# Own places for each activation form, and the forms of a short-conv layer made in two parts

## The chip, the cores and the metric

The kernel runs on one core of one Trainium2 chip. The metric is the device time of one execution in microseconds (us); the lower the better. The core has five engines that this text names as the profile does: PE (matrix multiply; PEld is its weight load), DVE (vector), ACT (scalar and activation), POOL (GpSimd) and SP (which here only issues transfers). Each has its own queue of instructions and takes them strictly in order; an instruction that waits holds up all that stand behind it on the same engine. Transfers (DMA) are issued from SP's queue and, where a transfer adds to what is already in its target, from POOL's.

## The reference

A decoder trunk of two layers on 512 positions (T) of 2048 features, in float32, with a final RMS norm:

```python
for layer in range(DEPTH):                      # DEPTH = 2
    hn = rmsnorm(h, norm_w[layer])
    if layer % 2 == 0:
        h = h + hybrid_layer(hn, ...)           # DeltaNet heads and windowed attention
    else:
        h = h + shortconv_layer(hn, ...)
return rmsnorm(h, final_norm_w)

def shortconv_layer(h, w_in, conv_w, w_out):
    gate_b, gate_c, u, z = jnp.split(h @ w_in, 4, axis=-1)   # 4 x 3072 columns
    y = gate_b * causal_depthwise_conv(gate_c * u, conv_w)
    return (y * jax.nn.silu(z)) @ w_out
```

The change touches the seam between the two layers (the output projection of layer 1 and the input projection of layer 2) and the seam between layer 2's input and output projection.

## The kernel before

Features lie on the 128 partitions, so activations are 16 tiles of 128x512 (m or k = 0..15). A float32 product is made of three faster ones: an operand is split into a high part (`hi`, rounded, made by ACT) and the remainder (`lo`, made by DVE), and `mm3` issues hi·hi, hi·lo and lo·hi. Weights come in chunks of eight k tiles (128x1024, 512 KB): a load into `w_raw`, then `w_hi` on ACT and `w_lo` on DVE, three places each.

**Output projection of layer 1** (lines 787 to 837). For each of the 16 m tiles, PE accumulates 24 k tiles; `made` adds the residual tile `rx` (that gives h1), stores it to `H1d` in DRAM, squares it (`sq` on ACT) and adds the square to `ssq` on DVE, from which layer 2's norm factor comes. m = 14 and 15 run together as `last`, with k outside. Layer 2's own activation input is `hs`, h1 times the norm weight (`scaled`, ACT); the norm factor itself (`rbc`) is multiplied in later. For this factor PE makes two small products, `rs_ps` (from `ssq`) and, after a step on DVE and one on POOL (`rs_k`), `rs_pb`; a list of tasks with due times (`flow`) puts them between the products of the first pair.

**Input projection of layer 2** (lines 839 to 941). The 3072 channels are 24 tiles; for each tile two `pair`s make two of the four projections each. A pair splits positions and k tiles in two halves and makes its two outputs by seven products (0 to 6) instead of eight. A product is 24 matmuls of 128x256: for each of eight j one `fm` tile, that is a sum or difference of quarters of `hs[2j]` and `hs[2j+1]`, split into hi and lo. `forms` makes all seven `fm` tiles of a j (56 in all; each takes an ACT and a DVE step, and the sums `fa` to `fd` run on DVE). They stay in place for all 48 pairs. The order of products on PE is 0, 5, 6, 4, 1, 2, 3, into the banks acc, sb, sc, sb, acc, sb, sc. Their weights are five raw chunks q11, s1, s3, q12, q22, of which s1 and s3 each get a second load added to them by a transfer that POOL issues; product 0 uses q11, product 5 q11+s1, product 6 s3.

In `made`, the forms of j = 0, 1, 2 and 7 (m < 6 and m ≥ 14) come straight from h1. For j = 3 to 6 the kernel reads h1 back from `H1d` into `hr` (two places, shared with `sq`), while the last two m tiles are on PE: eight loads of 256 KB and eight `hs`.

**Places before.** Splits of layer 1's activations and half the forms share one set of 32 places ("x"), the rest of the forms 24 places ("x2"). The results of layer 2's mixer, `y`, go to `Y2d`; behind the last pair 23 of them are read back as `yl` (six places, shared with the channel tiles `ct`), split by `split_y` into places of "x" and "x2", and the final projection runs over them.

PE's order is the program's order. The order on the other engines is set by a scheduler at build time from the program's order and priorities (`high_priority` moves weight loads and splits ahead); on the chip it is fixed.

Of the kernel before, what the change touches and what calls it, by code (L numbers as in the profile page):

```python
# [7 lines left out]
F32 = mybir.dt.float32  # L8
# [23 lines left out]
NX2 = 24  # L32
NJ1 = 3
NRAW = 6
SPLIT_AHEAD = 600

# [38 lines left out]
def hybrid_trunk(ctx: ExitStack, tc: tile.TileContext, xT, w1, w1o, w2, w2o, nw, dcw, scw, hp, dnw, cst, msk, rope,  # L75
# [120 lines left out]
    def split_x(pool, tag, bufs, src, k, layer):  # L196
        hi = pool.tile([P, T], F32R, name="x_hi", tag=tag, bufs=bufs)
        lo = pool.tile([P, T], F32R, name="x_lo", tag=tag, bufs=bufs)
# [6 lines left out]
    with tc.tile_pool(name="ini", bufs=3) as ini:  # L205
# [11 lines left out]
        for k in range(KT):  # L217
# [5 lines left out]
            xs1.append(split_x(xp, "x", 32, xr, k, 0))  # L223
# [346 lines left out]
    with tc.tile_pool(name="dn", bufs=2, side="right") as dn:  # L570
# [166 lines left out]
        PX, PYD = (xp, "x", 32), (yd, "yd", 17)  # L737
        ys = [None] * KO

        def split_ready():  # L740
            for i, yt in enumerate(ytiles):
                if ys[i] is None and yt is not None:
                    ys[i] = split_y(PX if i < 16 else PYD, yt)
# [28 lines left out]
    def forms(pool, j, he, ho):  # L772
        e1, e2, o1, o2 = he[:, 0:H], he[:, H:T], ho[:, 0:H], ho[:, H:T]
        form(0, j, e1)
        fa, fb = (pool.tile([P, H], F32, name=n) for n in ("fa", "fb"))
        V.tensor_tensor(fa, e1, e2, op=ALU.subtract)
        V.scalar_tensor_tensor(fb, fa, -1.0, o2, op0=ALU.mult, op1=ALU.subtract)
        form(5, j, fb)
        form(4, j, fa)
        fc, fd = (pool.tile([P, H], F32, name=n) for n in ("fa", "fb"))  # L780
        V.tensor_tensor(fc, e2, o2, op=ALU.subtract)
        form(6, j, fc)
        form(1, j, o1)
        form(2, j, o2)
        V.tensor_tensor(fd, o1, fb, op=ALU.add)
        form(3, j, fd)

    with tc.tile_pool(name="op1", bufs=2, side="right") as op1:
# [50 lines left out]
    with tc.tile_pool(name="w4", bufs=1) as w4, tc.tile_pool(name="sc", bufs=1, side="right") as sc:  # L839
# [27 lines left out]
        def pair(wa, wb, c1, c2):  # L867
# [10 lines left out]
            with tc.high_priority(offset=SPLIT_AHEAD):  # L878
                w = split_w(q11)
            product(w, 0, a, True)  # L880
            a1 = sc.tile([P, H], F32, name="a1", bufs=2)
            A.activation(a1, a[:, 0:H], AF.Copy)
            with tc.high_priority(offset=SPLIT_AHEAD):
                V.tensor_tensor(q11, q11, s1, op=ALU.add)
                w = split_w(q11)
            product(w, 5, b, True)
            e = sc.tile([P, H], F32, name="e", bufs=2)
            V.tensor_tensor(e, b[:, 0:H], a1, op=ALU.add)
            with tc.high_priority(offset=SPLIT_AHEAD):
                w = split_w(s3)  # L890
            product(w, 6, c, True)
# [20 lines left out]
        def ctile(w=T):  # L912
            return sc.tile([P, w], F32, name="ct", tag="ct", bufs=6)

        rbc2 = sc.tile([P, T], F32, name="rbc2")
        for c in range(NCH):
# [3 lines left out]
            pair(w2[4 * c], w2[4 * c + 1], cc, u)  # L920
# [20 lines left out]
        ys = [None] * NCH  # L941
        for c in range(NCH):
            if c < NCH - 1:
                yl = sc.tile([P, T], F32, name="yl", tag="ct", bufs=6)
# [3 lines left out]
            ys[c] = split_y(PX if c < 16 else (x2p, "x2", NX2), yl)  # L948
# [129 lines left out]
```

## Time and profile before

| | us |
|---|---|
| median of 3 runs | 2817.7 |
| lowest and highest run | 2816.68 and 2822.33 |
| the profiled execution, its own time | 2821.6 |
| its span, first to last instruction | 2819.8 |
| PE busy | 2774.8 (98%) |
| DVE busy | 1798.9 (64%) |
| ACT busy | 1091.6 (39%) |
| POOL busy | 160.6 (6%) |

Times in the trace count from the start of the span. A matmul's start is firm; its end is modelled and overlaps the next one's start, so the distance between starts is what a matmul costs. An entry such as `[5.47 <-ACT w_hi L851]` says that the engine sat idle for 5.47 us before this instruction and that the instruction at line 851 of ACT released it. PEclk is the clock that PE was granted, as a share of 2.4 GHz.

### The profile page before, as it was taken

What the parts mean: (1) busy time and instruction counts of PE and PEld (TensorE: products, weight loads), DVE (VectorE), ACT (ScalarE), POOL (GpSimd) and SP (SyncE); (2) the same over time, 40 slices, a digit from 0 to 9 for tenths busy, and PEclk for the clock granted to TensorE, in tenths of its full rate; (3) what the DMA queues carried; (4) which work ended last, traced back from release to release, by engine and by line L of the source; (5) the groups of instructions that cost most, each with busy time, mean ns of one, the idle gap of its engine ahead of it and who ended that gap; (6) DMA issues with size and microseconds to landing.
All of it is one profiled execution on the core that took longest, in us unless ns stands there. A gap on an engine that the chain in (4) does not pass through costs nothing.

```text
span 2819.8 us, 41852 instructions
## 1 busy us (share of the span) xinstructions
PE 2774.8 (98%) x16648; PEld 2463.6 (87%) x16648; DVE 1798.9 (64%) x2707; ACT 1091.6 (39%) x1803; POOL 160.6 (6%) x226
## 2 busy tenths in 40 slices
PE   8999999999999999999999899999999999999998
PEld 6888888888887888888887899999999999997887
DVE  7766999555445655665334677777777777774223
ACT  5443444444432323234323444444444444443221
POOL 3110000000000000000000100000000000000000
PEclk9999999999999999999999999999999999999999
DMA  5655223322224333333444767776677676754333
GB/s 170 183 169 186 90 87 127 111 88 86 94 86 127 124 105 110 115 113 112 127 127 135 217 181 200 186 204 182 190 191 197 187 191 188 194 164 141 114 112 112
DMA packets 163059, 410.58 MB, mean 146 GB/s; under 512 B 41184, under 2 KB 55776, under 8 KB 162608
## 3 DMA queue, kind: packets, MB, share of 16 engines
q1 hardware_dynamic: 149040, 357.57, 39.4%
q0 software_dynamic: 13824, 50.34, 10.1%
q8 instruction: 131, 2.15, 0.3%
q14 instruction: 64, 0.52, 0.1%
HBM read 373.44 MB, written 34.41 MB: 145 GB/s over the span
## 4 chain that ended last, share of the span: by engine, by line
PE 93%; DVE 3%; DMA 2%; issue 1%; ACT 1%; SPq 0%; DVEq 0%; POOL 0%; ACTq 0%; POOLq 0%
PE acc L151 17%; PE acc L153 17%; PE acc L152 17%; PE sb L862 5%; PE sb L864 5%; PE sb L863 5%; PE sc L862 3%; PE sc L864 3%; PE acc L862 3%; PE acc L864 3%; PE sc L863 3%; PE acc L863 3%; PE p L96 2%; DMA w_raw<-in_w_dram 1%; DVE w_lo L146 1%
## 5 line engine op out<-in xcount | busy, mean ns | idle before, releaser
L151 PE MATMUL acc<-x_hi,w_hi 128*128 128x512 f32 x1536 | 622.5, 405 | 1.6 <-DVE cv_raw L319 1.6
L153 PE MATMUL acc<-x_hi,w_lo 128*128 128x512 f32 x1536 | 602.3, 392 | 5.1 <-DVE w_lo L146 5.1
L152 PE MATMUL acc<-x_lo,w_hi 128*128 128x512 f32 x1536 | 600.6, 391 | 0.5 <-DVE x_lo L200 0.3
L144 ACT ACTIVATE w_hi<-w_raw 128x1024 fp32r<-128x1024 f32 (+2 forms) x302 | 308.9, 1024 | 683.9 <-PE acc L152 513.9
L851 ACT ACTIVATE w_hi<-w_raw 128x1024 fp32r<-128x1024 f32 x336 | 356.3, 1061 | 559.2 <-PE acc L863 165.8
L146 DVE TENSOR_TENSOR w_lo<-w_raw,w_hi 128x1024 fp32r<-128x1024 f32 (+2 forms) x302 | 363.6, 1206 | 315.1 <-ACT w_hi L144 314.4
L853 DVE TENSOR_TENSOR w_lo<-w_raw,w_hi 128x1024 fp32r<-128x1024 f32 x336 | 411.0, 1224 | 160.9 <-ACT w_hi L851 159.0
L153 PEld LDWEIGHTS acc<-x_hi,w_lo 128*128 128x128 f32 x1536 | 289.2, 188 | 69.6 <-DVE w_lo L146 7.2
L151 PEld LDWEIGHTS acc<-x_hi,w_hi 128*128 128x128 f32 x1536 | 290.1, 189 | 57.4 <-DVE cv_raw L319 1.8
L152 PEld LDWEIGHTS acc<-x_lo,w_hi 128*128 128x128 f32 x1536 | 290.3, 189 | 55.8 <-DVE x_lo L200 1.8
L862 PE MATMUL sb<-fm,w_hi 128*128 128x256 f32 x1152 | 325.9, 283 | 0.0
L864 PE MATMUL sb<-fm,w_lo 128*128 128x256 f32 x1152 | 325.2, 282 | 0.0
L863 PE MATMUL sb<-fm,w_hi 128*128 128x256 f32 x1152 | 324.5, 282 | 0.0
L151 PE MATMUL acc<-y_hi,w_hi 128*128 128x512 f32 (+1 forms) x792 | 307.6, 388 | 4.8 <-ACT y_hi L732 3.2
L152 PE MATMUL acc<-y_lo,w_hi 128*128 128x512 f32 (+1 forms) x792 | 305.7, 386 | 3.5 <-DVE y_lo L734 3.5
L153 PE MATMUL acc<-y_hi,w_lo 128*128 128x512 f32 (+1 forms) x792 | 305.8, 386 | 1.2 <-DVE w_lo L146 1.2
L862 PE MATMUL sc<-fm,w_hi 128*128 128x256 f32 x768 | 218.0, 284 | 5.5 <-ACT w_hi L851 5.5
L862 PEld LDWEIGHTS sb<-fm,w_hi 128*128 128x128 f32 x1152 | 219.7, 191 | 0.0
L863 PEld LDWEIGHTS sb<-fm,w_hi 128*128 128x128 f32 x1152 | 218.9, 190 | 0.0
L864 PEld LDWEIGHTS sb<-fm,w_lo 128*128 128x128 f32 x1152 | 218.5, 190 | 0.0
L864 PE MATMUL sc<-fm,w_lo 128*128 128x256 f32 x768 | 217.5, 283 | 0.5 <-DVE w_lo L853 0.5
L863 PE MATMUL acc<-fm,w_hi 128*128 128x256 f32 x768 | 216.0, 281 | 1.3 <-DVE fm L769 1.3
(241 smaller groups left out, 4322.5 us busy)
## 6 DMA issues: line engine op xcount, KB each, us to landing
w_raw<-in_w_dram SPq DMA_DIRECT2D x428, 512.0 KB, 4.4
w_raw<-in_w_dram POOLq DMA_DIRECT2D x96, 512.0 KB, 7.1
w_raw<-in_w1o_dram SPq DMA_DIRECT2D x48, 512.0 KB, 3.6
w_raw<-in_w2o_dram SPq DMA_DIRECT2D x48, 512.0 KB, 3.6
Y2d<-y SPq DMA_DIRECT2D x23, 256.0 KB, 5.3
yl<-Y2d SPq DMA_DIRECT2D x23, 256.0 KB, 4.4
xr<-in_xT_dram SPq DMA_DIRECT2D x16, 256.0 KB, 4.3
KQd<-kq SPq DMA_DIRECT2D x8, 512.0 KB, 5.1
```

The source lines that it names most:

```text
L96: PE.matmul(o, lhsT, rhs, start=start, stop=stop)
L144: A.activation(hi, raw, AF.Copy)
L146: V.tensor_sub(lo, raw, hi.bitcast(F32))
L151: PE.matmul(acc, hi, xh, start=first, stop=False)
L152: PE.matmul(acc, hi, xl, start=False, stop=False)
L153: PE.matmul(acc, lo, xh, start=False, stop=last)
L851: A.activation(hi, src, AF.Copy)
L853: V.tensor_sub(lo, src, hi.bitcast(F32))
L862: PE.matmul(o, hi[:, j, :], xh, start=first and j == 0, stop=False, skip_group_check=not first)
L863: PE.matmul(o, hi[:, j, :], xl, start=False, stop=False, skip_group_check=not first)
L864: PE.matmul(o, lo[:, j, :], xh, start=False, stop=j == NJ - 1, skip_group_check=not first)
```

## The change

There are five edits. (1) Splits and forms get places of their own: for each of the seven forms eight places (`homes`), four sets in the pool that layer 1's splits use and three in the other. (2) `made` now makes forms 0, 5 and 6 (`EARLY`) for every pair of m tiles straight from h1, not only for four of them. Forms 4 and 1, and then 2 and 3 (`LATE`), are made in two passes over j = 0..6, both of which read h1 back: 28 `hr` loads and 28 `hs` in place of eight and eight. j = 7 has all seven forms made from h1 as before. (3) The first pair (`early`) runs products 0, 5 and 6 over j = 0..6 first and j = 7 of the three afterwards. (4) The store of h1 for m = 14 and 15 stands behind its square. (5) Channel tiles `ct` have four places instead of six, `yl` has three of its own, and the final splits take the places of forms 0, 5, 6, 4, 1, 2 in that order.

```diff
-NX2 = 24
-NJ1 = 3
+CT = 4
...
-    slots = iter([(x2p, "x2", NX2)] * NX2 + [(xp, "x", 32)] * 32)
+    EARLY, LATE = (0, 5, 6), (4, 1, 2, 3)
+    homes = [(x2p, "f0"), (xp, "x1"), (xp, "x2"), (xp, "x3"), (xp, "x0"), (x2p, "f1"), (x2p, "f2")]
...
-            if m < 2 * NJ1 or m >= KT - 2:
-                scaled(m, h1)
-                if m % 2:
-                    forms(op1, m // 2, hs[m - 1], hs[m])
-            SP.dma_start(H1d[m], h1)
+            scaled(m, h1)
+            if m % 2:
+                forms(op1, m // 2, hs[m - 1], hs[m], EARLY if m < KT - 1 else EARLY + LATE)
+            if m < KT - 2:
+                SP.dma_start(H1d[m], h1)
             sq = op1.tile([P, T], F32, name="sq1", tag="hr")
             A.activation(sq, h1, AF.Square)
             V.tensor_tensor(ssq, ssq, sq, op=ALU.add)
+            if m >= KT - 2:
+                SP.dma_start(H1d[m], h1)
...
-        for j in range(NJ1, NJ - 1):
-            for m in (2 * j, 2 * j + 1):
-                hr = op1.tile([P, T], F32, name="hr", tag="hr")
-                SP.dma_start(hr, H1d[m])
-                scaled(m, hr)
-            forms(op1, j, hs[2 * j], hs[2 * j + 1])
+        for which in (LATE[:2], LATE[2:]):
+            for j in range(NJ - 1):
+                for m in (2 * j, 2 * j + 1):
+                    hr = op1.tile([P, T], F32, name="hr", tag="hr")
+                    SP.dma_start(hr, H1d[m])
+                    scaled(m, hr)
+                forms(op1, j, hs[2 * j], hs[2 * j + 1], which)
...
+            else:
+                for js in (range(NJ - 1), range(NJ - 1, NJ)):
+                    for w, f, o in ((wa0, 0, a), (wb0, 5, b), (wc0, 6, c)):
+                        product(w, f, o, True, js)
...
-            return sc.tile([P, w], F32, name="ct", tag="ct", bufs=6)
+            return sc.tile([P, w], F32, name="ct", tag="ct", bufs=CT)
...
-                yl = sc.tile([P, T], F32, name="yl", tag="ct", bufs=6)
+                yl = sc.tile([P, T], F32, name="yl", bufs=3)
...
-            ys[c] = split_y(PX if c < 16 else (x2p, "x2", NX2), yl)
+            ys[c] = split_y(homes[FREED[c // 4]] + (NJ,), yl)
```

Line numbers move: what was line 831 (the `hr` load) is 842 in the changed kernel, 872 and 873 (the loads of q11 and s3) are 883 and 884, 870 (s1) is 881, 851 (`w_hi`) is 862, 795 (`hs`) is 803, 862 to 864 (the matmuls of a product) are 873 to 875.

The first place is SP's queue at the end of layer 1's output projection. Before, the last `hr` load stands ahead of q11 (line 872); s3 and seven more weight chunks come behind it, then the stores of h1:

```order
L831 DMA hr<-H1d 128x512
L872 DMA w_raw<-in_w_dram 128x1024
L873 DMA w_raw<-in_w_dram 128x1024
L875 DMA w_raw<-in_w_dram 128x1024
L876 DMA w_raw<-in_w_dram 128x1024
L870 DMA w_raw<-in_w_dram 128x1024
L872 DMA w_raw<-in_w_dram 128x1024
L873 DMA w_raw<-in_w_dram 128x1024
L804 DMA H1d<-rx 128x512 x2
```

In the changed kernel q11 (line 883) stands behind the 14th `hr` load and s3 (line 884) behind the 20th:

```order
L842 DMA hr<-H1d 128x512 x6
L883 DMA w_raw<-in_w_dram 128x1024
L842 DMA hr<-H1d 128x512 x6
L884 DMA w_raw<-in_w_dram 128x1024
L886 DMA w_raw<-in_w_dram 128x1024
L887 DMA w_raw<-in_w_dram 128x1024
L881 DMA w_raw<-in_w_dram 128x1024
L883 DMA w_raw<-in_w_dram 128x1024
L884 DMA w_raw<-in_w_dram 128x1024
L842 DMA hr<-H1d 128x512 x2
L817 DMA H1d<-rx 128x512 x2
L842 DMA hr<-H1d 128x512 x2
```

Two `hr` loads now stand behind s3 and five more chunks, and the last six (two of them shown) behind the stores; each `hr` load waits for the `hs` that read its place two loads earlier.

The second place is ACT's queue at the same point. Before, `w_hi` of q11 and of q11+s1 is followed at once by the scaling of m = 14 and 15 (`hs<-rx`) and their squares:

```order
L851 ACTIVATE w_hi<-w_raw 128x1024 x2
L795 ACTIVATE hs<-rx,nw_sb 128x512
L806 ACTIVATE sq_12784<-rx 128x512
L795 ACTIVATE hs<-rx,nw_sb 128x512
L806 ACTIVATE sq_12820<-rx 128x512
L768 ACTIVATE fm<-hs 128x256
L768 ACTIVATE fm<-fb 128x256
L768 ACTIVATE fm<-fa 128x256 x2
L768 ACTIVATE fm<-hs 128x256 x2
```

In the changed kernel the rows begin with the 21st `hs<-hr` and `w_hi` of s3; eight rows are left out, and then come the last `hs<-hr`:

```order
L803 ACTIVATE hs<-hr,nw_sb 128x512
L862 ACTIVATE w_hi<-w_raw 128x1024
...
L767 ACTIVATE fm<-fb 128x256
L803 ACTIVATE hs<-hr,nw_sb 128x512 x2
L803 ACTIVATE hs<-rx,nw_sb 128x512
L814 ACTIVATE sq_12928<-rx 128x512
L803 ACTIVATE hs<-rx,nw_sb 128x512
L767 ACTIVATE fm<-hs 128x256
L814 ACTIVATE sq_12964<-rx 128x512
```

The scaling of m = 14 and 15 and both squares now stand behind all 28 `hs<-hr`, and so behind all 28 loads; so do the forms of j = 7.

The third place is PE's order in the first pair. Before, `rs_ps` stands within product 5 (bank sb) and `rs_pb` within product 6 (bank sc):

```order
L863 MATMUL sb<-fm,w_hi 128x256
L864 MATMUL sb<-fm,w_lo 128x256
L96 MATMUL rs_ps<-cst_sb,ssq 128x128 x4
L862 MATMUL sb<-fm,w_hi 128x256
L863 MATMUL sb<-fm,w_hi 128x256
L864 MATMUL sb<-fm,w_lo 128x256
...
L864 MATMUL sc<-fm,w_lo 128x256
L96 MATMUL rs_pb<-cst_sb,rs_k 128x128 x4
L862 MATMUL sc<-fm,w_hi 128x256
```

In the changed kernel `rs_ps` stands between j = 0..6 of product 5 and j = 0..6 of product 6, and `rs_pb` ahead of the three j = 7:

```order
L874 MATMUL sb<-fm,w_hi 128x256
L875 MATMUL sb<-fm,w_lo 128x256
L95 MATMUL rs_ps<-cst_sb,ssq 128x128 x4
L873 MATMUL sc<-fm,w_hi 128x256
L874 MATMUL sc<-fm,w_hi 128x256
...
L875 MATMUL sc<-fm,w_lo 128x256
L95 MATMUL rs_pb<-cst_sb,rs_k 128x128 x4
L873 MATMUL acc<-fm,w_hi 128x256
L874 MATMUL acc<-fm,w_hi 128x256
L875 MATMUL acc<-fm,w_lo 128x256
L873 MATMUL sb<-fm,w_hi 128x256
```

The 21 matmuls of product 6 for j = 0..6 now all stand behind `rs_ps`, where only those of j = 6 and 7 of product 5 and the whole of product 6 did before.

## Rows read from the trace of the kernel before

**Rows 1.** The page: share of the chain that ended last, by engine.

```profile
PE 93%; DVE 3%; DMA 2%; issue 1%; ACT 1%; SPq 0%; DVEq 0%; POOL 0%; ACTq 0%; POOLq 0%
```

**Rows 2.** Window of the pairs: us; PE, PEld, DVE, ACT, POOL busy (x); PEclk, DMA, GB/s.

```profile
1600.00:2500.00 900.00, 900.00 (x7545) 900.00 (x7544) 696.50 (x831) 385.25 (x449) 80.07 (x112) 1.00 0.71 191
```

**Rows 3.** Waits of PE, 1545 to 1600.

```profile
PE sc L862 <- ACT w_hi L851: 5.5, 1, 5.5
PE acc L863 <- DVE fm L769: 1.3, 1, 1.3
```

**Rows 4.** Timeline of PE, 1549 to 1577: start, duration, line, tiles, idle before.

```profile
1549.73 0.39 PE L153 MATMUL acc<-y_hi,w_lo 128*128 128x512 f32 x1
1549.96 0.28 PE L862 MATMUL acc<-fm,w_hi 128*128 128x256 f32 x1
1550.07 0.28 PE L863 MATMUL acc<-fm,w_hi 128*128 128x256 f32 x1
...
1558.57 1.05 PE L96 MATMUL rs_ps<-cst_sb,ssq 128*128 128x128 f32 x8
```

**Rows 5.** Timeline of DVE, 1555 to 1576 (same columns).

```profile
1575.98 0.42 DVE L896 TENSOR_TENSOR b<-sb,a 128x256 f32<-128x256 f32 x1 [0.61 <-PE sb L864]
```

**Rows 6.** Windows of 1549.9 to 1600 (columns as rows 2).

```profile
1558.40:1565.20 6.80, 1.94 (x17) 1.73 (x16) 0.16 (x1) 0.50 (x1) 2.20 (x3) 1.00 1.05 311
1565.20:1572.00 6.80, 5.73 (x25) 5.43 (x26) 4.96 (x5) 2.88 (x5) 0.74 (x2) 0.50 1.02 255
```

**Rows 7.** Timeline of SP's queue, 1510 to 1575; one issue a row, or several (x).

```profile
1513.31 0.56 SPq L831 DMA_DIRECT2D hr<-H1d  x1
...
1529.30 0.33 SPq L831 DMA_DIRECT2D hr<-H1d  x1
...
1550.15 0.33 SPq L873 DMA_DIRECT2D w_raw<-in_w_dram  x1
...
1553.49 0.87 SPq L804 DMA_DIRECT2D H1d<-rx  x2
```

**Rows 8.** The tile hr, 1505 to 1560: its instructions and landings.

```profile
L795 ACT ACTIVATE hs<-hr,nw_sb x8: 705/717/725, 1516.4 to 1533.5; 128x512 f32<-128x512 f32 x8
...
DMA to landing us min/median/max: 2.5/3.0/4.7
```

**Rows 9.** The tile w_raw, 1539 to 1560: landings of its loads.

```profile
DMA to landing us min/median/max: 3.6/8.1/12.0
```

**Rows 10.** Timeline of ACT, 1548 to 1576.

```profile
1550.83 0.62 ACT L806 ACTIVATE sq<-rx 128x512 f32<-128x512 f32 x1
...
1564.70 2.95 ACT L851 ACTIVATE w_hi<-w_raw 128x1024 fp32r<-128x1024 f32 x3 [9.13 <-DMA w_raw<-in_w_dram]
```

**Rows 11.** Timeline of POOL, 1530 to 1580.

```profile
1560.39 1.35 POOL L188 TENSOR_TENSOR rs_k<-rs_t,mhalf 128x4 f32<-128x4 f32 x1
```

**Rows 12.** Waits of PE, 2500 to 2600.

```profile
PE acc L152 <- DVE y_lo L734: 3.5, 7, 0.9
PE acc L151 <- ACT y_hi L732: 3.2, 4, 1.3
```

**Rows 13.** Window of the final projection's first tile (columns as rows 2).

```profile
2526.57:2556.60 30.03, 23.26 (x75) 15.05 (x74) 20.56 (x31) 16.00 (x26) 0.00 (x0) 0.89 0.78 258
```

**Rows 14.** The tile yl, 2490 to 2560.

```profile
L732 ACT ACTIVATE y_hi<-yl x23: 612/630/634, 2522.2 to 2551.0; 128x512 fp32r<-128x512 f32 x23
L734 DVE TENSOR_TENSOR y_lo<-yl,y_hi x23: 684/689/695, 2523.2 to 2551.7; 128x512 fp32r<-128x512 f32 x23
...
DMA to landing us min/median/max: 2.7/4.4/6.7
```

**Rows 15.** Timeline of POOL, 1900 to 1950.

```profile
1905.59 0.44 POOL L918 MEMSET ct<- 128x2 f32 x1
1922.91 0.86 POOL L871 DMA_DIRECT2D w_raw<-in_w_dram  x1 [16.88 <-DMA w_raw<-in_w_dram]
```

**Rows 16.** Timeline of DVE, 1905 to 1924.

```profile
1911.39 0.74 DVE L928 SCALAR_TENSOR_TENSOR ct<-ct,scw_sb 128x512 f32<-128x512 f32 x1
```

More of the change, by code (lines that the diff above doesn't have):

```diff
@@ L194, in rstd_task, with split_x @@
         done.append(pb)
-    def split_x(pool, tag, bufs, src, k, layer):
-        hi = pool.tile([P, T], F32R, name="x_hi", tag=tag, bufs=bufs)
-        lo = pool.tile([P, T], F32R, name="x_lo", tag=tag, bufs=bufs)
+    def split_x(src, k, layer):
+        hi, lo = (xp.tile([P, T], F32R, name=n, tag=f"x{k // 4}", bufs=8) for n in ("x_hi", "x_lo"))
         A.activation(hi, src, AF.Copy, scale=nw_sb[:, layer, k:k + 1])
@@ L742, in split_ready @@
                 if ys[i] is None and yt is not None:
-                    ys[i] = split_y(PX if i < 16 else PYD, yt)
+                    ys[i] = split_y((xp, f"x{i // 4}", 8) if i < 16 else PYD, yt)
         flow.until(lambda: all(t is not None for t in ytiles[:KO - 2]))
@@ L761, in hybrid_trunk @@
     rd2 = []
-    slots = iter([(x2p, "x2", NX2)] * NX2 + [(xp, "x", 32)] * 32)
+    EARLY, LATE = (0, 5, 6), (4, 1, 2, 3)
+    homes = [(x2p, "f0"), (xp, "x1"), (xp, "x2"), (xp, "x3"), (xp, "x0"), (x2p, "f1"), (x2p, "f2")]
     fm = [[None] * NJ for _ in range(7)]
     def form(i, j, src):
-        pool, tag, bufs = next(slots)
-        t = pool.tile([P, 2, H], F32R, name="fm", tag=tag, bufs=bufs)
+        pool, tag = homes[i]
+        t = pool.tile([P, 2, H], F32R, name="fm", tag=tag, bufs=NJ)
         A.activation(t[:, 0, :], src, AF.Copy)
@@ L770, in form, with forms @@
         fm[i][j] = (t[:, 0, :], t[:, 1, :])
-    def forms(pool, j, he, ho):
+    def forms(pool, j, he, ho, which):
         e1, e2, o1, o2 = he[:, 0:H], he[:, H:T], ho[:, 0:H], ho[:, H:T]
-        form(0, j, e1)
+        if 0 in which:
+            form(0, j, e1)
         fa, fb = (pool.tile([P, H], F32, name=n) for n in ("fa", "fb"))
         V.tensor_tensor(fa, e1, e2, op=ALU.subtract)
[L777 to L786, printed above, removed]
+        if 5 in which or 3 in which:
+            V.scalar_tensor_tensor(fb, fa, -1.0, o2, op0=ALU.mult, op1=ALU.subtract)
+        if 5 in which:
+            form(5, j, fb)
+        if 6 in which:
+            fc = pool.tile([P, H], F32, name="fa")
+            V.tensor_tensor(fc, e2, o2, op=ALU.subtract)
+            form(6, j, fc)
+        if 4 in which:
+            form(4, j, fa)
+        if 1 in which:
+            form(1, j, o1)
+        if 2 in which:
+            form(2, j, o2)
+        if 3 in which:
+            fd = pool.tile([P, H], F32, name="fb")
+            V.tensor_tensor(fd, o1, fb, op=ALU.add)
+            form(3, j, fd)
     with tc.tile_pool(name="op1", bufs=2, side="right") as op1:
@@ L854, in split_w, with product @@
             return hi, lo
-        def product(w, f, o, first):
+        def product(w, f, o, first, js=range(NJ)):
             hi, lo = w
             o = o[:, 0:H]
-            for j in range(NJ):
+            for j in js:
                 flow.poll()
@@ L865, in product, with pair @@
                 flow.t += 0.36
-        def pair(wa, wb, c1, c2):
+        def pair(wa, wb, c1, c2, early=False):
             with tc.high_priority(offset=SPLIT_AHEAD):
@@ L919, in hybrid_trunk @@
             u = cu[:, 2:T + 2]
-            pair(w2[4 * c], w2[4 * c + 1], cc, u)
+            pair(w2[4 * c], w2[4 * c + 1], cc, u, c == 0)
             if c == 0:
```

32 lines of the change are left out of this document (20 added, 12 removed).

## The prediction

> **What bounds the kernel now.** I read the share of the chain first: PE holds 93% of it [rows 1]. Then PE's windows: over the 900 us of the pairs shown PE is busy for all 900, at full clock [rows 2]. So an edit can win or lose time only where PE waits, and I looked for these places in PE's waits. Two bear on the change.
>
> The first is the seam into layer 2. The first matmul of the first pair starts at 1549.96 [rows 4], and product 4, the fourth, has ended when DVE takes its bank at 1575.98 [rows 5]: 26.0 us. Matmuls of 128x256 start 0.11 to 0.12 us apart [rows 4]; four products of 24 at 0.12 us are 11.5 us, and the two small norm products take 1 us each (`rs_ps`, 1.05 [rows 4]). Some 12.5 us are lost here. In the waits, 5.5 of it is product 6 waiting for `w_hi` of s3, and 1.3 is a form of j = 7 [rows 3]; the rest is the clock, 0.50 from 1565.2 to 1572.0 behind the long wait, and before it [rows 6]. s3 is late because its load is issued only at 1550.15, when layer 1's last matmul gives its memory free [rows 7], and lands, with its second load added, for the `w_hi` at 1564.70 [rows 10].
>
> The second is the final projection's first tile. 75 matmuls of 128x512 take 30.03 us [rows 13]; such matmuls start 0.23 us apart [rows 4], so 17 us would do: 13 us are lost, in waits for `y_lo` and `y_hi` [rows 12] and in a mean clock of 0.89 [rows 13].
>
> **The change part by part.**
>
> *Fewer forms behind h1 of m = 15, and j = 7 put last.* It is meant for the 1.3 us wait, and removes it: j = 7 comes last. At most it gives 1.3 us [rows 3], if nothing else is late.
>
> *28 loads in place of eight.* This moves far more. Two places hold `hr`, and a load waits for the `hs` two before it, so the loads pace themselves. Before, eight were issued from 1513.31 to 1529.30 [rows 7], seven steps of 2.28 us. The floor is two in flight, landing in 2.5 us and read in 0.72 us [rows 8]: 1.6 us each; with the median landing of 3.0 us it is 1.9 us and some overhead. I take 2.1 us, since weight loads and a wait for the places of layer 1's splits fall into the first loads but not into those behind 1540; bounds 1.6 and 2.28.
>
> *s3 behind the 20th load.* The 20th is issued at 1513.3 + 19 x 2.1 = 1553.2, and s3 behind it, in SP's queue, 3 us later than before (0 at a rate of 1.6, 6.5 at 2.28).
>
> *The loads behind the weights.* The 21st and 22nd load stand behind s3 and five more chunks. Before, the issue of these six and what follows took from 1550.15 to 1553.49 [rows 7], 3.3 us, and a chunk took up to 12.0 us to land, where one alone took 3.6 us [rows 9]; the DMA engines were busy throughout (share 1.05 and 1.02) [rows 6]. Two more loads at the tail of six would be issued at about 1556.5 and land some 12 us later, at 1568.5, when s3 with its addition is there too. Bounds: 2.5 us, if they do not queue [rows 8], and 15 us.
>
> *The last six.* They go in three rounds of two, each round two times 2.1 us: 12.6 us. The 28th `hs` ends at about 1569.5 + 12.6 = 1582. Meanwhile PE has nothing: products 0 and 5 over j = 0..6 are 42 matmuls, 5 us, and their end at about 1557 to 1558 leaves PE at `rs_ps`, whose `ssq` needs the squares of m = 14 and 15; these stand on ACT behind the 28th `hs`. Product 6 stands behind `rs_ps` on PE, so it waits as well, although its weights and six forms are long there.
>
> *From the last `hs` to product 4's end.* Two `hs` and two squares on ACT (0.72 and 0.62 us each [rows 8, 10]) and the last addition to `ssq` on DVE: 3.5 us, 1585.5. `rs_ps`, 1 us. Then 21 matmuls of product 6: PE has stood still for some 28 us, and after 5.5 us it had 0.50 of its clock for 6.8 us [rows 3, 6], so at twice 0.12 us they take 5 us. `rs_k` on POOL (1.35 us [rows 11]) is hidden by them. `rs_pb` and nine matmuls of j = 7: 2 us. That makes 1593.5. The three places for split weights are held until j = 7 of the products, so product 4's `w_hi` (some 1 us: three in 2.95 [rows 10]) starts only as j = 7 of product 0 ends: 1 us more. 24 matmuls: 2.9 us. Product 4 ends at about 1597.5, against 1575.9 before: **+22 us**. With the low bounds throughout it is +8 (worked out under the rivals), with the high ones (s3 6.5 us late in place of 3, landings of 15 us, rounds of 4.6 us) some +30 to 33. Behind it nothing is late: the next pair's loads have 14 us of products 4, 1, 2 and 3 to arrive in.
>
> A page of the Trainium skill, "DMA: Bandwidth & Descriptors", section "Anatomy of one DMA — SWDGE (gpsimd) path", gives a transfer a fixed 2.0 us and its bytes at 436 GB/s. For 256 KB that is 2.6 us, and the lowest landing, 2.5 us [rows 8], agrees. By this rule alone all 28 loads would keep that pace and the sum would be the rival's +8. Its section "Queues, rings and completion order" says that an engine takes what a queue hands it in ring order, so that a load behind six chunks comes after their bytes; the landings of up to 12.0 us [rows 9] speak for the second rule here.
>
> *Own places for the final splits.* `split_y` starts when the first product of the last pair gives form 0 free, some 13 us before the first `y_hi` at 2522.2 [rows 14] (the last pair's six later products and a little more). But `yl` now has three places where it had six. A place is held for the landing (2.7 to 6.7, median 4.4), `y_hi` 0.63 and `y_lo` 0.69 [rows 14], with 0.3 us between: 6.0 us for three, 2.0 a tile. Three tiles are there early; the other 20 take 40 us from about 2509.5, to 2549.5, where the last `y_lo` ended at 2552.4 before. So **-3 us**. Bounds: 0, if loads of weights for the final projection and their splits on ACT stand in the way, and -13, the whole loss [rows 13], which needs landings near 2.7 us (1.45 us a tile, done at 2538).
>
> *ct with four places.* Four channel tiles a channel make each wait for its reader of the channel before. The nearest case is POOL's memset: at 1905.59 it ran a channel ahead, now it waits for line 928 on DVE, which ends at 1912.1 [rows 15, 16]. Queued behind it on POOL are the additions to weights; the next is issued at 1922.91 [rows 15]. 10 us of slack hide the wait: 0. Without it each of 23 channels could lose some us.
>
> *The rest* (more `hs` and forms inside the output projection, names of places for layer 1's splits): 0, with the 1.3 us of one late form [rows 3] either way.
>
> The sum on the profiled execution is 2821.6 + 22 - 3 = 2840.6. The runs' median lies 3.9 us below that execution's own time, so on the median it is 2817.7 + 19 = 2836.7. I predict 2837 us. A measurement of this kernel tells 0.2%, 5.6 us, from no change.
>
> **The rivals.**
> - *The forecast*: `hr` loads queue behind s3's group and the norm's squares behind all of them; 2829 to 2844.
> - *A slower chain*: the rate stays 2.28 us or worse, s3 goes out at 1557 or later, and each step behind it slips; middle +30, end 0 to -3: about 2847. For it speaks the rate before; against it, that DMA has little else to do from 1540 to 1550.
> - *Not slower*: behind s3 the loads land in 2.5 us. Issued at 1553.5, they give `hs` 21 and 22 at 1557.5, and three rounds of 2.5 + 1.4 us the 28th at 1569.2; `ssq` at 1572.7, product 6 at half clock to 1578.7, j = 7 to 1580.7, product 4 to 1584.5: +8. The same quick landings give `yl` its 1.45 us and the end its -11: 2815, no change that can be measured. It decides by the landing of the loads behind the six chunks; below 5 us it holds. Against it stand the 12.0 us [rows 9].
> - *Faster*: the early splits save all 13 us and the seam costs nothing: 2817.7 - 13 = 2805. That needs the squares of m = 14 and 15 by 1558, so 28 loads read by 1554.5, 1.5 us each without a stop; the lowest landings allow 1.6, and the queue behind s3 speaks against it.
>
> **How the numbers follow.** The forecast has 0.68, the slower chain 0.17, no change 0.09, faster 0.06. The two first are both slower: slower 0.85, same 0.09, faster 0.06. The likeliest one's own range is 2829 to 2844; for 8 in 10 I go from 2822 (the forecast with an end gain of 11 and 15 in the middle) to 2852 (the slower chain with no gain at the end).
>
> **What would show it.** In the profile of the changed kernel: PE idle for 20 us or more ahead of `rs_ps`, released by DVE's addition to `ssq`, in the waits near 1557 to 1586; `hr` landings of about 10 us for the 21st and 22nd load; a last `hs<-hr` near 1582; the clock at 0.50 behind it; the first `y_hi` near 2507 plus what the middle lost, and the last one only some us closer to the final projection's start than before. No PE wait between. I am wrong if PE's idle time ahead of `rs_ps` is below 10 us, if product 6 waits for forms, or if the channels show waits of their own.

## The result: 1.1% slower, and where the time went

The changed kernel takes 2850.4 us in the median (2848.74 to 2853.18) against 2817.6 for the kernel before: the ratio is 1.0114, with a 95% interval of 1.0097 to 1.0132. That lies at the upper edge of the predicted range of 2822 to 2852, on the side forecast, 13 us above the 2837 of the forecast, and above the 2829 to 2844 that the prediction gave its own theory. The changed kernel's profiled execution took 2848.74 us.

PE's waits of the changed kernel from 1500 to 1650 (engine, tile and line, what it waited for; total, times, longest) answer to [rows 3]:

```profile
PE rs_ps L95 <- DVE ssq L815: 30.6, 1, 30.6
PE sb L873 <- ACT w_hi L862: 3.4, 1, 3.4
PE sb L873 <- DVE e L913: 2.2, 1, 2.2
PE sb L875 <- DVE w_lo L864: 1.7, 1, 1.7
```

One wait of 30.6 us has come in: `rs_ps` for the squares of m = 14 and 15. The 5.5 us wait of product 6 for s3 is gone, since product 6 comes later than s3 now. The next three rows are small: product 5 waits 3.4 and 1.7 us, both ahead of the long wait, and product 4 2.2 us behind it.

Why the squares are late is in SP's queue (answering to [rows 7]) and ACT's (to [rows 8, 10]), here of the changed kernel:

```profile
1515.48 0.43 SPq L842 DMA_DIRECT2D hr<-H1d  x1
...
1545.79 10.25 SPq L842 DMA_DIRECT2D hr<-H1d  x6
1556.09 0.42 SPq L884 DMA_DIRECT2D w_raw<-in_w_dram  x1
...
1558.89 1.29 SPq L884 DMA_DIRECT2D w_raw<-in_w_dram  x1
1560.28 1.21 SPq L842 DMA_DIRECT2D hr<-H1d  x2
1562.42 1.63 SPq L817 DMA_DIRECT2D H1d<-rx  x2
1575.53 1.88 SPq L842 DMA_DIRECT2D hr<-H1d  x2
...
1580.94 4.51 SPq L842 DMA_DIRECT2D hr<-H1d  x4
```

```profile
1561.32 0.42 ACT L767 ACTIVATE fm<-fb 128x256 fp32r<-128x256 f32 x1 [1.49 <-DVE fb L793]
1574.78 0.72 ACT L803 ACTIVATE hs<-hr,nw_sb 128x512 f32<-128x512 f32 x1 [13.04 <-DMA hr<-H1d]
...
1580.19 1.35 ACT L803 ACTIVATE hs<-hr,nw_sb 128x512 f32<-128x512 f32 x2 [1.03 <-DMA hr<-H1d]
...
1583.71 1.39 ACT L803 ACTIVATE hs<-hr,nw_sb 128x512 f32<-128x512 f32 x2 [0.48 <-DMA hr<-H1d]
...
1588.89 0.72 ACT L803 ACTIVATE hs<-hr,nw_sb 128x512 f32<-128x512 f32 x1 [2.10 <-DMA hr<-H1d]
1590.27 0.72 ACT L803 ACTIVATE hs<-hr,nw_sb 128x512 f32<-128x512 f32 x1 [0.66 <-DMA hr<-H1d]
1590.90 0.71 ACT L803 ACTIVATE hs<-rx,nw_sb 128x512 f32<-128x512 f32 x1
...
1592.95 0.61 ACT L814 ACTIVATE sq<-rx 128x512 f32<-128x512 f32 x1
```

The reread loads go out from 1515.48, the 20th just ahead of s3 at 1556.09; the 21st and 22nd stand behind s3 and five chunks at 1560.28 and are read from 1574.78, after 13.04 us in which ACT did nothing; the other six take until 1590.27. Only then come the two `hs<-rx` and their squares. PE's `rs_ps` starts at 1594.52, 3.5 us after the last `hs<-hr` has ended; the clock granted from 1558.3 to 1599.2, a stretch in which PE is idle for most of the time, was 0.50 (columns as rows 2):

```profile
1558.30:1599.20 40.90, 9.10 (x41) 8.80 (x42) 17.46 (x43) 16.05 (x33) 4.67 (x6) 0.50 0.71 203
```

The wait shows in the chain of the whole execution too; on the page, `hr<-H1d` now holds 2% of it (a line of part 4):

```profile
PE acc L150 17%; PE acc L152 17%; PE acc L151 17%; PE sb L873 5%; PE sb L875 5%; PE sb L874 5%; PE sc L873 3%; PE acc L873 3%; PE sc L875 3%; PE acc L875 3%; PE sc L874 3%; PE acc L874 3%; PE p L95 2%; DMA hr<-H1d 2%; DMA w_raw<-in_w_dram 1%; PE o_ps L95 1%
```

The end, windows of the final projection's first tile in the changed kernel (columns as rows 2), and the tile `yl`, answering to [rows 13, 14]:

```profile
2556.36:2583.60 27.24, 21.67 (x75) 14.74 (x74) 16.25 (x24) 12.24 (x19) 0.00 (x0) 0.87 0.61 215
```

```profile
L730 ACT ACTIVATE y_hi<-yl x23: 613/629/634, 2537.4 to 2580.6; 128x512 fp32r<-128x512 f32 x23
L732 DVE TENSOR_TENSOR y_lo<-yl,y_hi x23: 683/686/694, 2539.3 to 2581.3; 128x512 fp32r<-128x512 f32 x23
...
DMA to landing us min/median/max: 2.6/3.5/5.2
```

The first tile's 75 matmuls take 27.24 us in place of 30.03; the first split starts 18.9 us ahead of the projection's first matmul (2537.4 against 2556.36), where it had started 4.4 us ahead. The last one is hardly earlier: 2580.6, 24.2 us behind that matmul, against 24.4 before.

Starts of PE's matmuls at a few marks split the profiled execution of each kernel into stretches; the medians are of all its runs. Matmul 200 is the start of PE's 200th matmul. Seam is from the first matmul of the first pair to the first of its fifth product; end is from the first matmul of the final projection's first tile to the first of its second.

| kernel | median, us | matmul 200 | start of the first pair | seam | end |
|---|---|---|---|---|---|
| before | 2817.6 | 57.8 | 1549.96 | 25.82 | 29.85 |
| changed | 2850.4 | 61.3 | 1550.59 | 56.81 | 27.06 |
| mid | 2853.0 | 64.4 | 1554.61 | 56.34 | 26.75 |
| one_pass | 2826.5 | 65.7 | 1559.62 | 28.93 | 27.72 |
| one_not_early | 2820.2 | 61.9 | 1552.18 | 25.22 | 27.14 |
| act_queue | 2856.2 | 63.3 | 1557.65 | 58.88 | 28.19 |
| reread_ahead | 2848.7 | 63.3 | 1554.09 | 55.83 | 27.81 |
| yl_shared | 2849.8 (one run) | 63.2 | 1553.32 | 56.16 | 25.75 |
| names_only | 2823.8 | 61.7 | 1554.84 | 25.69 | 28.17 |
| ct_yl_only | 2816.7 | 58.0 | 1549.39 | 25.85 | 25.63 |
| s3_later | 2820.4 | 58.4 | 1552.14 | 29.74 | 25.50 |
| stores_only | 2815.3 | 58.0 | 1547.24 | 25.31 | 25.28 |
| stores_first | 2809.2 | 58.0 | 1546.18 | 18.71 | 26.23 |

From before to changed the seam costs 31.0 us and the end gives back 2.8. The pairs in between give 1.8 us (922.02 us from the third pair's first matmul to the last pair's last, 920.19 in the changed kernel). The first pair starts 0.6 us later. These make 27.0 us, and the two profiled executions differ by 27.1 (2848.74 against 2821.6). The end is less certain than the seam, as it differs between traces of kernels with the same places there: 28.17 and 29.85 us with the places of before, 26.75 to 28.19 in the six with those of the changed kernel. The kernel before, run beside the others, had medians of 2817.6 to 2819.8.

### The profile page after: what moved, and what is told of

It reads as the page before. It is cut to its first block, busy times and chain, and to the rows that moved or that the text cites. A ratio compares the mean times of both kernels' runs of the same rounds, so it can differ in the third digit from the quotient of the medians.

```text
span 2846.9 us, 41954 instructions
## 1 busy us (share of the span) xinstructions
PE 2771.2 (97%) x16648; PEld 2459.8 (86%) x16648; DVE 1806.4 (63%) x2728; ACT 1111.4 (39%) x1831; POOL 161.2 (6%) x226
## 4 chain that ended last, share of the span: by engine, by line
PE 92%; DMA 4%; DVE 2%; ACT 1%; issue 0%; SPq 0%; DVEq 0%; POOL 0%; ACTq 0%
PE acc L150 17%; PE acc L152 17%; PE acc L151 17%; PE sb L873 5%; PE sb L875 5%; PE sb L874 5%; PE sc L873 3%; PE acc L873 3%; PE sc L875 3%; PE acc L875 3%; PE sc L874 3%; PE acc L874 3%; PE p L95 2%; DMA hr<-H1d 2%; DMA w_raw<-in_w_dram 1%; PE o_ps L95 1%
## 5 line engine op out<-in xcount | busy, mean ns | idle before, releaser
L873 PE MATMUL sc<-fm,w_hi 128*128 128x256 f32 x768 | 217.0, 283 | 0.0
L874 PE MATMUL sc<-fm,w_hi 128*128 128x256 f32 x768 | 216.4, 282 | 0.0
```

Of the source, the lines that this page charges most:

```text
L873: PE.matmul(o, hi[:, j, :], xh, start=first and j == 0, stop=False, skip_group_check=not first)
L874: PE.matmul(o, hi[:, j, :], xl, start=False, stop=False, skip_group_check=not first)
```

## The experiments

**mid**: all of `made` for m = 14 and 15 (scaling, forms of j = 7, squares, stores) moved between the two passes, so that the squares stand ahead of the second.

```diff
         for which in (LATE[:2], LATE[2:]):
             for j in range(NJ - 1):
...
+            if which == LATE[:2]:
+                for m, acc, rx in zip(last, accs, rxs):
+                    made(m, acc, rx)
-        for m, acc, rx in zip(last, accs, rxs):
-            made(m, acc, rx)
```

> The changed kernel with one move: m = 14 and 15 are scaled and squared between the two passes over the reread tiles, so their squares stand ahead of the second pass on ACT. Theory A (the second pass's 14 loads, put behind s3's group of weight chunks, are the cost, whoever waits for them): the 30.6 us wait of the norm product goes, but the second pass ends no earlier than 1590, and what needs it or stands behind it on ACT (the copy of product 0's bank, the forms of products 2 and 3) makes PE wait 20 us or more at product 4 or 2; 2840 to 2856. Rival B (only the place of the two squares on ACT is the cost): PE waits for s3 alone, as before the change; 2812 to 2822.

2853.0 us, ratio to before 1.0117 (1.0102 to 1.0132). PE's waits in mid, 1500 to 1650:

```profile
PE sb L874 <- DVE e L914: 28.2, 1, 28.2
PE sc L874 <- ACT w_hi L863: 9.2, 1, 9.2
```

`rs_ps` no longer waits. Product 4 waits 28.2 us instead, for `e`, which needs the copy of product 0's bank; that copy stands on ACT behind all 28 `hs<-hr`. The seam is as long as before the move (56.3 us). So the place of the squares is not the cost; the second pass is, and whatever stands behind it on ACT waits. Theory A holds, rival B falls.

**one_pass**: one pass that makes all four late forms, 14 loads.

```diff
-        for which in (LATE[:2], LATE[2:]):
+        for which in (LATE,):
```

> The changed kernel with one pass over the reread tiles that makes forms 4, 1, 2 and 3 together: 14 loads in place of 28, all of them ahead of s3 in SP's queue. Theory A (the number of loads and their place behind s3 are the cost): the last of them is read by about 1555, the norm product waits under 3 us, the seam loses about what it lost before the change, and the end keeps its 3 us; 2812 to 2822. Rival C (the order of the first pair with j = 7 last, and the split weights held for it, are the cost): still 2835 or more.

2826.5 us, ratio 1.0022 (1.0012 to 1.0033): 24 us below the changed kernel, and 4.5 above the upper end expected. PE's waits in one_pass, 1500 to 1650:

```profile
PE sc L873 <- ACT w_hi L862: 9.4, 1, 9.4
PE sb L873 <- DVE e L913: 2.2, 1, 2.2
...
PE rs_ps L95 <- DVE ssq L815: 0.3, 1, 0.3
```

`rs_ps` waits 0.3 us; the 30.6 us are gone with the second pass. The seam is bound by s3 again (9.4 us), and it still loses 3.1 us more than before, 2.2 of them at product 4, for `e`. The rest of the excess lies ahead of the first pair, which starts at 1559.6; but this profiled execution, of 2830.96 us, was the slowest of the eight.

**one_not_early**: one_pass, with products 0, 5 and 6 run whole in the first pair.

```diff
-            pair(w2[4 * c], w2[4 * c + 1], cc, u, c == 0)
+            pair(w2[4 * c], w2[4 * c + 1], cc, u)
```

> The changed kernel with one pass over the reread tiles and with products 0, 5, 6 in the first pair run whole again, j = 7 in its turn, not last. Theory H (with s3 as the bound of the seam, putting j = 7 last buys nothing): the seam from the first matmul of the pair to the end of the fourth product stays within 2 us of the 28.9 us of the one-pass kernel, or gets shorter by up to 3, since the places of split weights and the copy of bank acc come free before s3 arrives; 2821 to 2828. Rival I (j = 7 last is what keeps PE fed): 3 us or more longer; 2829 to 2834.

2820.2 us, ratio 1.0004 (0.9995 to 1.0013), below what was expected. The seam is 25.2 us, 3.7 shorter than in one_pass, where up to 3 was expected. PE's waits, 1545 to 1600:

```profile
PE sc L873 <- ACT w_hi L862: 6.9, 1, 6.9
PE acc L874 <- DVE fm L768: 0.9, 1, 0.9
PE acc L873 <- ACT fm L767: 0.8, 1, 0.8
```

The forms of j = 7 cost 1.7 us in all, as the 1.3 us of [rows 3] did, but they lie in time that is lost to s3 anyway (6.9 us). With j = 7 last, the split weights of three products are held and the copy of bank acc comes after the wait for s3. Theory H holds, rival I falls: beside one pass, edit 3 costs time.

**names_only**: the kernel before with other names for the same places.

```diff
-            xs1.append(split_x(xp, "x", 32, xr, k, 0))
+            xs1.append(split_x(xp, f"x{k // 4}", 8, xr, k, 0))
...
-                    ys[i] = split_y(PX if i < 16 else PYD, yt)
+                    ys[i] = split_y((xp, f"x{i // 4}", 8) if i < 16 else PYD, yt)
...
-    slots = iter([(x2p, "x2", NX2)] * NX2 + [(xp, "x", 32)] * 32)
+    slots = iter([(x2p, "x2", NX2)] * NX2 + [(xp, f"x{i // 8}", 8) for i in range(32)])
...
-            ys[c] = split_y(PX if c < 16 else (x2p, "x2", NX2), yl)
+            ys[c] = split_y((xp, f"x{c // 4}", 8) if c < 16 else (x2p, "x2", NX2), yl)
```

> The kernel before with nothing changed but the names of the 32 places that layer 1's splits and half the forms share: four sets of eight, in the same rotation, so that every tile keeps the place it had. At build time the scheduler orders the first 50 us otherwise with these names (as it does in the changed kernel). Theory F (this order costs the changed family its 3.4 to 7.8 us in the first 60 us): PE's 200th matmul starts at 61 to 66 us, in place of 58.1, and the whole is 2820 to 2826. Rival G (those us are differences between single executions): start near 58, 2817 to 2820, no change.

2823.8 us, ratio 1.0018 (1.0009 to 1.0027): 5.1 us slower, 2.5 to 7.6 by the interval. Windows of 20 to 60 us (columns as rows 2), first of the kernel before, then of names_only, then of the changed kernel:

```profile
20.00:60.00 40.00, 38.51 (x175) 30.88 (x176) 32.41 (x43) 21.27 (x36) 13.98 (x12) 1.00 0.49 168
```

```profile
20.00:60.00 40.00, 36.31 (x158) 28.74 (x159) 28.67 (x34) 19.51 (x34) 14.75 (x12) 0.96 0.48 165
```

```profile
20.00:60.00 40.00, 37.66 (x160) 30.01 (x161) 28.84 (x36) 20.02 (x34) 14.76 (x12) 0.93 0.50 170
```

In the same 40 us PE issues 175 matmuls in the kernel before, 158 with the new names, 160 in the changed kernel. By the rotation of the names no tile has another place or another reader. The order on PE is the same; the scheduler puts loads and splits of the first 50 us in another order on SP, ACT and DVE, and some later ones too, near 880, 1275 and 1530 us. Theory F's own mark is the 200th matmul: 61.7 us in place of 57.8, where 61 to 66 was expected. By that mark all traces fall into two groups: 57.8 to 58.4 us in the five kernels with the old names, 61.3 to 65.7 in the eight with the new ones. Theory F holds.

**ct_yl_only**: the kernel before with edit 5's places alone.

```diff
-            return sc.tile([P, w], F32, name="ct", tag="ct", bufs=6)
+            return sc.tile([P, w], F32, name="ct", tag="ct", bufs=4)
...
-                yl = sc.tile([P, T], F32, name="yl", tag="ct", bufs=6)
+                yl = sc.tile([P, T], F32, name="yl", bufs=3)
```

> The kernel before with one part of the change: four places for channel tiles and three of their own for the reread mixer tiles. Theory A: no channel waits (PE idle between 1600 and 2500 stays at 0); the splits start where they did, and three places instead of six make the final projection's first tile 0 to 4 us longer; 2817 to 2822. Rival D (the four places hold up weights on POOL or DVE in each channel): 2825 or more.

2816.7 us, ratio 0.9986 (0.9976 to 0.9996). PE does not wait between 1600 and 2500, so four channel places cost nothing. The end is shorter by 4.2 us in the traces, where 0 to 4 longer was expected, and by the interval the whole is 1.1 to 6.8 us faster than the kernel before. The tile `yl` in ct_yl_only:

```profile
L732 ACT ACTIVATE y_hi<-yl x23: 614/630/637, 2508.0 to 2549.0; 128x512 fp32r<-128x512 f32 x23
...
L945 SPq DMA_DIRECT2D yl<-Y2d x20: 319/320/565, 2509.7 to 2546.3; - x20
```

The first split starts at 2508.0, 14.2 us earlier than in [rows 14], with the forms in their old, shared places. So what held the splits back was `yl`'s wait for channel tiles; the forms' own places were not needed for it.

**yl_shared**: the changed kernel with seven places shared by channel tiles and `yl`.

```diff
-CT = 4
+CT = 7
...
-                yl = sc.tile([P, T], F32, name="yl", bufs=3)
+                yl = sc.tile([P, T], F32, name="yl", tag="ct", bufs=CT)
```

> The changed kernel with channel tiles and reread mixer tiles in one set of seven places, in place of four and three. Theory J (three places of its own set the pace of the reread): up to seven tiles are in flight once the last channel is done, and the first tile of the final projection takes 20 to 25 us in place of 27.1. Rival K (waiting for the channel tiles' places costs more than the depth gives, as in the kernel before): 28 to 31 us. The seam stays as in the changed kernel (56 to 57 us), the whole at 2842 to 2854.

The end takes 25.75 us, between what the theory and the rival expected, and 2849.8 us in one run. The splits start only at 2554.0 here (the row below), 4.4 us ahead of the projection, and the end is still 1.3 us shorter than in the changed kernel. That is one trace, and the end with three places of their own ranges over 1.4 us among the traces above, so the run doesn't settle how much depth buys beside an early start. It does show that sharing takes the early start away.

```profile
L730 ACT ACTIVATE y_hi<-yl x23: 612/617/636, 2554.0 to 2581.1; 128x512 fp32r<-128x512 f32 x23
```

**act_queue** and **reread_ahead** ask what makes the second pass slow. act_queue issues the reread loads from ACT:

```diff
-                    SP.dma_start(hr, H1d[m])
+                    A.dma_start(hr, H1d[m])
```

> The changed kernel with the 28 reread loads issued from ACT's queue instead of SP's; nothing else in the order of the squares changes. s3's load no longer stands behind the 20th reread load and goes out near 1550.5 instead of 1556.1. Theory A with the queue as cause of the long landings: loads 21 and 22 land in under 8 us instead of 14, the last is read near 1578 to 1583, PE's wait shrinks by 7 to 12 us; 2838 to 2844. Rival E (the DMA engines' bandwidth sets the landing, whichever queue): the landings stay at 12 us or more, and only the 5 us of the earlier start are won or nothing; 2845 to 2852.

2856.2 us, ratio 1.0131 (1.0116 to 1.0146): no faster than the changed kernel (1.0097 to 1.0132, so whether it is slower stays open), and above both expectations. The pair itself starts 7 us later than in the changed kernel; s3 went out at 1557.84, right behind its first matmul (1557.65). The wait of `rs_ps` is 27.8 us. The landings of the reread loads, of the changed kernel and of act_queue:

```profile
DMA to landing us min/median/max: 2.5/3.3/14.8
```

```profile
DMA to landing us min/median/max: 2.6/4.0/8.7
```

The longest landing is 8.7 us, where the changed kernel has 14.8. But each load now waits in ACT's queue for the work ahead of it, and the last `hs<-hr` starts at 1598.9, 41 us behind the pair's first matmul, against 40 in the changed kernel.

reread_ahead raises the loads over the weights:

```diff
-                    hr = op1.tile([P, T], F32, name="hr", tag="hr")
-                    SP.dma_start(hr, H1d[m])
-                    scaled(m, hr)
-                forms(op1, j, hs[2 * j], hs[2 * j + 1], which)
+                    with tc.high_priority(offset=2 * SPLIT_AHEAD):
+                        hr = op1.tile([P, T], F32, name="hr", tag="hr")
+                        SP.dma_start(hr, H1d[m])
+                        scaled(m, hr)
+                with tc.high_priority(offset=2 * SPLIT_AHEAD):
+                    forms(op1, j, hs[2 * j], hs[2 * j + 1], which)
```

> The changed kernel with the reread loads, their scaling and their forms at a higher priority than the weights: in SP's queue the 21st and 22nd load then stand behind s3 and two chunks, not five. Theory A with the queue (a load lands only behind the chunks that stand ahead of it): these two land after 7 to 11 us in place of 14, the norm product's wait shrinks from 30.6 to 23 to 28 us; 2841 to 2848. Rival P (the bytes in flight set the landing, in whatever order they were issued): 13 us or more, the wait within 2 us of 30.6; 2848 to 2854.

2848.7 us, ratio 1.0113 (1.0099 to 1.0127). SP and ACT in reread_ahead:

```profile
1559.36 0.42 SPq L886 DMA_DIRECT2D w_raw<-in_w_dram  x1
...
1561.19 2.31 SPq L843 DMA_DIRECT2D hr<-H1d  x2
1563.55 0.67 SPq L883 DMA_DIRECT2D w_raw<-in_w_dram  x1
...
1568.40 0.96 SPq L843 DMA_DIRECT2D hr<-H1d  x2
```

```profile
1567.65 1.36 ACT L803 ACTIVATE hs<-hr,nw_sb 128x512 f32<-128x512 f32 x2 [2.16 <-DMA hr<-H1d]
...
1579.68 0.72 ACT L803 ACTIVATE hs<-hr,nw_sb 128x512 f32<-128x512 f32 x1 [4.53 <-DMA hr<-H1d]
```

Loads 21 and 22 stand behind three chunks now and are both read by 1569.0, so the first lands within 6.5 us of its issue. But 23 and 24, issued at 1568.40 behind the other three chunks and the stores, are read only from 1579.68 on. The wait of `rs_ps` stays at 29.7 us. So the theory was right on the landing and wrong on the wait and the time, and rival P the other way round: what stands ahead in the queue sets which load is late, and moving it saves nothing that can be measured. My reading, which no run isolates, is that the eight loads behind s3 have to come through beside the same chunks in either order.

**s3_later**, **stores_only** and **stores_first** go on from ct_yl_only to the seam's own bound, s3. s3_later runs product 6 after 4 and 1 in the first pair:

```diff
-            with tc.high_priority(offset=SPLIT_AHEAD):
-                w = split_w(s3)
-            product(w, 6, c, True)
+            if not late6:
+                product6()
...
+            if late6:
+                product6()
+                V.tensor_tensor(c2[:, H:T], c[:, 0:H], b2, op=ALU.subtract)
...
-            pair(w2[4 * c], w2[4 * c + 1], cc, u)
+            pair(w2[4 * c], w2[4 * c + 1], cc, u, c == 0)
```

> The kernel before with four channel places and three of their own for the reread mixer tiles (as in ct_yl_only), and with product 6, the one that needs s3, run after products 4 and 1 in the first pair. Theory L (s3's late landing is the bound of the seam in the kernel before): product 6's wait of 5.5 us shrinks below 2 us, its half clock goes with it, and the first four products take 4 to 8 us less; 2807 to 2813. Rival M (weights of the other products arrive as late, all being loaded behind layer 1's last matmul): the wait moves to product 4 or 1; 2814 to 2818.

2820.4 us, ratio 1.0004 (0.9995 to 1.0013), above both expectations. Product 6 no longer waits, but product 4 waits 12.3 us for `e`:

```profile
PE sb L862 <- DVE e L888: 12.3, 1, 12.3
```

ACT in s3_later shows why:

```profile
1572.98 0.38 ACT L882 ACTIVATE a<-acc 128x256 f32<-128x256 f32 x1 [5.12 <-DMA H1d<-rx]
```

The copy `a` of product 0's bank waits for the stores of h1: its memory is that of the `rx` tiles, which the stores still read. Theory L is right that s3 held product 6, and wrong that nothing stood behind it; rival M is right that the wait moves to product 4, and wrong on the cause, which is not a weight. stores_first adds an early issue of the two stores:

```diff
-            V.tensor_tensor(h1, acc, rx, op=ALU.add)
+            with tc.high_priority(offset=2 * SPLIT_AHEAD if m >= KT - 2 else 0):
+                V.tensor_tensor(h1, acc, rx, op=ALU.add)
...
-            SP.dma_start(H1d[m], h1)
+            with tc.high_priority(offset=2 * SPLIT_AHEAD if m >= KT - 2 else 0):
+                SP.dma_start(H1d[m], h1)
```

> As s3_later (kernel before, four channel places, three own for the reread, product 6 after 4 and 1 in the first pair), with the stores of h1 for m = 14 and 15 put ahead of the weight chunks behind s3 in SP's queue. In s3_later product 4 waited 12.3 us for e, because the copy of product 0's bank lies in memory that the two stores still read, and these land behind the chunks. Theory N (that place is the second bound of the seam): the wait for e falls below 2 us, product 6 waits under 3 us, and the first four products take 19 to 23 us in place of 25.9 (29.7 in s3_later); 2807 to 2813. Rival O (chunks and s3 come later by what the stores take): the wait moves to product 6 or 1, 25 us or more; 2814 to 2819.

2809.2 us, ratio 0.997 (0.9958 to 0.9981). PE's waits in stores_first, 1545 to 1640:

```profile
PE sb L864 <- DVE e L890: 2.6, 1, 2.6
PE acc L864 <- ACT fm L768: 1.3, 1, 1.3
PE acc L865 <- DVE fm L769: 0.8, 1, 0.8
```

The seam takes 18.7 us, 7.1 less than before the change. The wait for `e` is 2.6 us, a little above the 2 expected. This is the fastest kernel of the study, 9 us below the kernel before run beside it; part of that is the shorter end, which ct_yl_only has too. stores_only has the same stores with the products in their usual order:

> As ct_yl_only, with the stores of h1 for m = 14 and 15 ahead of the chunks behind s3, and the products in their usual order. Theory N: product 6 comes before product 4 and still waits for s3, which is issued ahead of the stores, so the first four products take 24 to 27 us as before; 2813 to 2818. Rival O: s3 or the chunks come later by the stores' time, 28 us or more; 2818 to 2822.

2815.3 us, ratio 0.9993 (0.9985 to 1.0002), seam 25.3 us: early stores alone buy only 0.5 us at the seam (25.85 in ct_yl_only), since product 6 still waits for s3:

```profile
PE sc L864 <- ACT w_hi L853: 7.4, 1, 7.4
```

The two edits pay only together: each removes a wait that hides the other's.

## Why the prediction was right, and what it missed

*The place and the mechanism* were as forecast: 28 loads two at a time, s3 behind the 20th, two loads behind s3's group, the squares behind all of them on ACT, PE idle at `rs_ps` until then. mid and one_pass show it: without the second pass the wait is gone; with the squares moved, product 4 waits 28.2 us in place of `rs_ps`. A 20 us wait or more was named as the mark; it is 30.6.

*The size* was off: the seam was put at +22 us and measured +31.0. The term that was too small is the arrival of the loads, 1582 for the end of the last `hs` against 1591.0. The rate was right: 19 steps of 2.12 us from the first load at 1515.48 to the 20th, 2.1 predicted. But s3 went out at 1556.1, not 1553.2, above all since the first load was 2.2 us later than in the rows of before; six chunks (s3 and five more; before, too, it is five behind s3 and not seven) took 4.2 us to issue, not 3.3; from the issue of the 21st load to its read it took 14.5 us, not 12 (the upper bound was 15); and from that read to the end of the 28th 16.2 us, not 13.5, in rounds of 5.4, 3.5 and 5.2 us where 4.2 each were put. These are 2.9, 0.9, 2.5 and 2.7 us, 9 in all. From the last `hs` to the fourth product's end I put 15.5 us and it took 16.5: `rs_ps` took 1.7 us at the half clock where 1 was put, product 6's 21 matmuls 3.9 where 5 were put, since the clock rose at 1599.2, and the wait ahead of product 4 was 2.2 where 1 was put.

The ring-order rule of the Trainium skill ("DMA: Bandwidth & Descriptors", section "Queues, rings and completion order") agrees with the landings: up to 14.8 us behind six chunks, 6.5 behind three, 8.7 at most from another queue. The same page's fixed-cost rule, by which the seam would have cost +8, is stated there for transfers issued from POOL, and these loads go out from SP; here it fits only the quickest landing, 2.5 us.

*The start* was put at 0 and the names of places were costed with "the rest". That step failed: names_only shows 5.1 us, 2.5 to 7.6. I had read the order of the first 50 us as harmless and had no row for it. At the first pair the two groups of kernels overlap (1550.6 to 1559.6 us with the new names, 1546.2 to 1552.1 with the old), so one pair of traces can hide the loss there, as before and changed do with 0.6 us between them. At the 200th matmul the groups are apart.

*The end* came out at -2.8 with -3 predicted, but not for the reason given, and by luck: traces of kernels with the same places at the end differ by 1.4 to 1.7 us there. I had the splits start early because the forms' places come free form by form. ct_yl_only has the early start without those places: it was `yl`'s wait for channel tiles that held it back, and three places of its own undo it. That three places then set the pace is not shown: the unchanged start of the last split speaks for it, and yl_shared doesn't settle it.

*ct with four places* cost 0, as forecast. *j = 7 last* was put at a gain of 1.3 us at most; one_not_early shows a loss of 3.7 at the seam beside one pass. What it costs in the changed kernel itself, beside the larger wait, was not measured. Edit 4, the stores behind the squares, has no run of its own.

The sum in the runs' terms: 31.0 for the seam, 5.1 for the start, -2.8 for the end, -1.8 for the pairs make 31.5, and 32.8 were measured between the medians. The start is taken from names_only here, since the profiled execution of the kernel before was 4 us slower than its median and shows only 0.6 of it. The pairs' 1.8 us were in no term of the prediction. The "slower chain" rival, at 2847, came nearer than the forecast, but its cause, a rate of 2.28 us or worse, was not what happened.

## What to carry to other kernels

A reread that saves memory must be counted in loads and in what it stands ahead of and behind in each queue: here twenty more loads put 31 us on the one thing that everything else waited for, and one pass in place of two took 28 of them back. Where two stalls overlap, as s3's and the stores' did, removing one gains next to nothing, and only the pair of edits pays. Renaming places can reorder a schedule far from the edit, so a change of names deserves a run of its own.

## What was not expected of the hardware

The pace of matmuls depends on where the moving operand lies (the one that runs past the loaded weights, here the form). In the changed kernel products 0, 5 and 6 read forms from one pool and 4, 1, 2 and 3 from the other. PE's timeline of the changed kernel shows it at the first matmuls of the second pair's products 0, 5, 6, 4, 1 and 2:

```profile
1616.04 0.28 PE L873 MATMUL acc<-fm,w_hi 128*128 128x256 f32 x1
...
1618.87 0.28 PE L873 MATMUL sb<-fm,w_hi 128*128 128x256 f32 x1
...
1621.70 0.28 PE L873 MATMUL sc<-fm,w_hi 128*128 128x256 f32 x1
...
1624.53 0.29 PE L873 MATMUL sb<-fm,w_hi 128*128 128x256 f32 x1
...
1627.41 0.28 PE L873 MATMUL acc<-fm,w_hi 128*128 128x256 f32 x1
...
1630.29 0.28 PE L873 MATMUL sb<-fm,w_hi 128*128 128x256 f32 x1
```

The first three products take 2.83 us each, the next two 2.88: 0.1178 and 0.1200 us a matmul of the same shape, at the same clock. The means over 44 pairs are the same: 2.83 three times, then 2.88 four times. In the kernel before each product mixes both pools, and all take 2.86 to 2.87 us. There the pace changes inside the product, where the pool does: at j = 4 in products 0, 5 and 4, at j = 3 in the other four, since the 24 places of "x2" are used up after three forms of j = 3. Ahead of the switch, from j = 1 on, starts are 0.1178 us apart; from the second j behind it they are 0.1200 apart. So it is the place and not the product that sets the pace.

This pace alone does not explain the pairs' 1.8 us, since both kernels have 24 of their 56 forms in the faster pool. What differs is how often a pair goes from one pool to the other and back: seven times before, once in the changed kernel. Each time adds 0.0067 us to the starts around it (means over 46 pairs), so six fewer save 0.040 us a pair, and 46 pairs 1.8 us. Why one place is faster, and why the switch costs time, was not tried.
